# Three mixed cells of eight in the up projection of a hybrid decoder layer, with the embedding's input split in the attention stage and two plain cells at the end of the first pair

## The chip, the cores and the metric

The kernel runs on one core of one Trainium2 chip. The metric is the device time of one execution in microseconds, the median of several runs. Below, PE is the TensorE engine (the matmuls), DVE is VectorE, ACT is ScalarE, POOL is GpSimd, and SP is the engine that issues the weight transfers.

## The reference

One layer of a decoder is computed in float32 for 256 tokens of width 2048:

```python
a = RMSNorm(h)
z, xBC, dt, q, k, v = split(a @ W_in)
h = h + concat(ssd_heads(z, xBC, dt), windowed_attention(q, k, v)) @ W_out
g, u = split(causal_dwconv3(RMSNorm(h) @ W_up))          # W_up: 2048 x 11264
h = h + (SiLU(g) * u) @ W_down                           # W_down: 5632 x 2048
h = h + sigmoid(RMSNorm(h) @ W_pg) * RMSNorm(p @ W_pe)   # p: 256 x 256, W_pe: 256 x 2048
```

The change lies in the line of `W_up`, and in the product `p @ W_pe` (the embedding), which the kernel computes early and keeps in memory.

## The kernel before

**Products.** A float32 product is made of three matmuls: each operand is split into a high part (a cast, on ACT) and a low part (source minus high, a subtraction on DVE), and hi·wh, hi·wl and lo·wh are accumulated in one PSUM bank. Each matmul has a 128x128 stationary piece of the activations and a 128x512 piece of the weights. Such a triple is called a run here.

**Weights.** They come in pieces of 512 KB (128 partitions x two k-tiles x 512 columns) on SP's queue into seven raw buffers. ACT casts a piece to `wh` (L205), DVE subtracts it to `wl` (L206); four such pairs are kept, and in the feed-forward stage a fifth. A raw buffer is free when both have read it, a pair when PE has used it.

**Order.** The order of PE's instructions is as the code is written (a manual schedule around it). The order on DVE, ACT, POOL and SP is set by a scheduler when the kernel is built, and each of these engines then works its rows in that order: a row that waits holds up all rows behind it.

**Stages.** The input projection with the SSD heads; the attention, whose work is handed out in numbered slots (`at`) between the chunks of the projection and of the output projection; then the feed-forward stage. This one begins with the embedding: its input `p` is loaded, split into `ph` and `pl`, and `embed(n)` (four of them, 12 matmuls each) multiplies it by `W_pe`; DVE copies each result out (L896) and it is stored. Between them stand `norm(n)` (scaling of h) and `left(n)` (transposes on PE at L932, and the split left operands of four k-tiles: for plain cells at L209, for mixed ones the sums at L943).

**Pairs and cells.** The up projection runs in 11 pairs, `up(c)`: 512 columns of g and 512 of u, each summed over 2048 rows, which are cut in eight cells `kp` of 256 rows. A *plain* cell is 8 runs (24 matmuls) and needs two weight pieces split. A *mixed* cell does the same 2x2 block product with seven block products instead of eight (sums of blocks, after Winograd): 7 runs (21 matmuls), but before that four subtractions 128x512 on DVE to make `ta` and `tb` from two raw pieces (L962), and three and a half pieces to split (`g`, `v` of half size, `ta`, `tb`). Cells 0 and 4 are mixed, the others plain.

**Banks.** A pair uses all eight PSUM banks: P1, P5, P6, P7 only for mixed cells, Q22 only for plain ones, Q2, Q3, Q4 for both. After the last mixed cell the P banks are combined in SBUF (L1029 to L1033), after the last plain cell the four Q banks are added (L1035). A bank can be used by the next pair once DVE has read it. Then `finish` turns the result (a copy on ACT L1000, a transposing transfer, a copy on ACT L1003), and the short convolution (ACT L307, DVE L309), SiLU and the product follow; all that runs beside the next pair.

**Between pairs.** `down` (the product with `W_down`) of an earlier group of pairs stands between two pairs from the third on; between pairs 0 and 1, and between 1 and 2, nothing stands. Pair 0 is special: `left` is made inside it (`boundary`), and its plain cells come first, so its order is 1, 2, 3, 5, 6, 7, 0, 4. The other pairs go 0 to 7.

## Time and profile before

| what | value |
|---|---|
| runs | 1433.77 us median of 3 (1432.09 to 1439.97) |
| the profiled execution | 1435.36 us, of which the span in the trace is 1433.6 us |
| TensorE clock granted, mean over the span | 0.995 of full |
| PE busy | 1414.3 us, 6461 matmuls |
| DVE busy | 1110.3 us, 1480 instructions |
| ACT busy | 901.6 us, 1196 instructions |
| feed-forward stage begins | 603.10 us is the start of the last matmul of the output projection |
| pairs 2 to 10 | from about 723 us on |

Times in the trace are microseconds from the start of the span. A row of a timeline gives start, busy time, engine, line, operation, output and inputs, and in brackets how long the engine was idle before it and which instruction ended the wait. A row of a group gives the total busy time and the mean time of one in ns. A row of a stretch gives, for PE, PE's weight loads, DVE, ACT and POOL, the busy time and the count, then the mean granted clock of PE, the share of the DMA engines and GB/s. Instructions on one engine overlap a little, so the pitch of neighbours (start to start) is shorter than the duration of one.

### The profile page before, as it was taken

Reading aid. Unit: us, or ns where it says so; the run is one execution under the profiler, and the core shown is the slowest. Engines: PE = TensorE matmul, PEld = TensorE weight load, DVE = VectorE, ACT = ScalarE, POOL = GpSimd, SP = SyncE. Lnnn points to the kernel's source line nnn. Section 1 sums busy time; section 2 is a strip of 40 time slices with the busy share of each in tenths; the row PEclk is TensorE's granted clock in tenths of the full one; section 3 lists DMA queues with packets and bytes.
Section 4 is the critical chain, followed back from the end, with each engine's and each line's share of the span. In section 5 each row is a group of like instructions: output and inputs, shape, how many; then the busy total and the mean of one; then the engine's idle time right before and its main releaser. Section 6 shows DMA issues by size and latency. Waiting matters only on the chain.

```text
span 1433.6 us, 18135 instructions
## 1 busy us (share of the span) xinstructions
PE 1414.3 (99%) x6461; PEld 1156.6 (81%) x6461; DVE 1110.3 (77%) x1480; ACT 901.6 (63%) x1196; POOL 131.5 (9%) x114
## 2 busy tenths in 40 slices
PE   9999999999999999898999999999999999999998
PEld 7888888888787778686888888888888888888887
DVE  7678876776778888688898887878788787877764
ACT  6675555644677666565787575666757576665653
POOL 0002010018344522000000000000000000000000
PEclk9999999999999999999999999999999999999999
DMA  9656655548777778565678677686766777676672
GB/s 340 232 173 207 208 184 184 162 151 231 191 208 200 205 224 227 180 229 157 191 221 219 226 213 210 217 228 199 220 216 185 239 215 214 204 222 214 219 253 67
DMA packets 164907, 296.80 MB, mean 207 GB/s; under 512 B 93201, under 2 KB 96081, under 8 KB 164177
## 3 DMA queue, kind: packets, MB, share of 16 engines
q1 hardware_dynamic: 162800, 289.94, 67.7%
q10 hardware_dynamic: 2016, 5.72, 1.1%
q8 instruction: 50, 0.82, 0.2%
q14 instruction: 41, 0.33, 0.1%
HBM read 270.41 MB, written 4.23 MB: 192 GB/s over the span
## 4 chain that ended last, share of the span: by engine, by line
PE 64%; DVE 4%; ACT 1%; issue 1%; DMA 0%; POOL 0%; DVEq 0%; ACTq 0%
PE b L951 10%; PE b L950 10%; PE b L952 10%; PE b L241 8%; PE b L243 8%; PE b L242 8%; PE acc L241 3%; PE acc L242 3%; PE acc L243 3%; DVE wl L206 2%; PE tr L802 1%; ACT wh L205 0%; PE sc L761 0%; DMA w<-in_w_up_dram 0%; PE b L293 0%
## 5 line engine op out<-in xcount | busy, mean ns | idle before, releaser
L206 DVE TENSOR_TENSOR wl<-w,wh 128x1024 fp32r<-128x1024 f32 (+1 forms) x473 | 582.7, 1240 | 208.2 <-ACT wh L205 207.3
L205 ACT CAST wh<-w 128x1024 fp32r<-128x1024 f32 (+1 forms) x473 | 488.5, 1044 | 320.5 <-PE b L952 110.7
L950 PE MATMUL b<-wh,ah 128*128 128x512 f32 x484 | 189.6, 392 | 3.9 <-DVE c L1032 2.0
L951 PE MATMUL b<-wl,ah 128*128 128x512 f32 x484 | 188.9, 390 | 0.3 <-DVE wl L206 0.3
L952 PE MATMUL b<-wh,al 128*128 128x512 f32 x484 | 189.0, 390 | 0.0
L242 PE MATMUL acc<-wl,ah 128*128 128x512 f32 x448 | 176.9, 395 | 0.0
L241 PE MATMUL acc<-wh,ah 128*128 128x512 f32 x448 | 175.8, 395 | 0.0
L243 PE MATMUL acc<-wh,al 128*128 128x512 f32 x448 | 175.6, 392 | 0.0
L241 PE MATMUL b<-wh,gh 128*128 128x512 f32 x352 | 137.1, 390 | 0.0
L243 PE MATMUL b<-wh,gl 128*128 128x512 f32 x352 | 137.0, 389 | 0.0
L242 PE MATMUL b<-wl,gh 128*128 128x512 f32 x352 | 136.9, 389 | 0.0
L950 PEld LDWEIGHTS b<-wh,ah 128*128 128x128 f32 x484 | 91.3, 189 | 24.5 <-ACT wh L205 2.4
L951 PEld LDWEIGHTS b<-wl,ah 128*128 128x128 f32 x484 | 91.2, 189 | 19.5 <-DVE wl L206 0.7
L952 PEld LDWEIGHTS b<-wh,al 128*128 128x128 f32 x484 | 91.2, 188 | 19.0
L241 PE MATMUL acc<-wh,yh 128*128 128x512 f32 x256 | 101.2, 395 | 0.3 <-DVE h L417 0.3
L242 PE MATMUL acc<-wl,yh 128*128 128x512 f32 x256 | 99.8, 390 | 0.0
L243 PE MATMUL acc<-wh,yl 128*128 128x512 f32 x256 | 99.6, 390 | 0.0
L241 PEld LDWEIGHTS acc<-wh,ah 128*128 128x128 f32 x448 | 84.2, 188 | 18.9 <-issue 1.1
L242 PEld LDWEIGHTS acc<-wl,ah 128*128 128x128 f32 x448 | 84.2, 188 | 18.4 <-issue 1.1
L243 PEld LDWEIGHTS acc<-wh,al 128*128 128x128 f32 x448 | 84.2, 188 | 17.8 <-issue 0.7
L243 PEld LDWEIGHTS b<-wh,gl 128*128 128x128 f32 x352 | 66.1, 188 | 13.7
L242 PEld LDWEIGHTS b<-wl,gh 128*128 128x128 f32 x352 | 66.1, 188 | 13.7
(289 smaller groups left out, 2256.7 us busy)
## 6 DMA issues: line engine op xcount, KB each, us to landing
w<-in_w_up_dram SPq DMA_DIRECT2D x176, 512.0 KB, 4.4
w<-in_w_in_dram SPq DMA_DIRECT2D x126, 512.0 KB, 4.1
w<-in_w_down_dram SPq DMA_DIRECT2D x88, 512.0 KB, 4.3
w<-in_w_out_dram SPq DMA_DIRECT2D x64, 512.0 KB, 4.1
w<-in_w_pg_dram SPq DMA_DIRECT2D x32, 512.0 KB, 4.4
seg<-scr SPq DMA_DIRECT2D x8, 512.0 KB, 5.0
xt<-in_xT_dram SPq DMA_DIRECT2D x16, 128.0 KB, 6.9
h<-in_x_dram SPq DMA_DIRECT2D x2, 1024.0 KB, 7.7
```

Of the source, the lines that this page charges most:

```text
L205: S.copy(hi, src)
L206: V.tensor_tensor(out=lo, in0=src, in1=hi.bitcast(F32), op=ALU.subtract)
L241: PE.matmul(acc[b], lhsT=hi, rhs=wh[:, i, :], start=(k == 0), stop=False)
L242: PE.matmul(acc[b], lhsT=hi, rhs=wl[:, i, :], start=False, stop=False)
L243: PE.matmul(acc[b], lhsT=lo, rhs=wh[:, i, :], start=False, stop=(k == total - 1 or (b == NB - 1 and k + 1 == whole)))
L802: PE.matmul(v3(o[e * HD : (e + 1) * HD, kv * 2 * P : (kv + 1) * 2 * P], 2), lhsT=v[kb][:, vs], rhs=pT[e][:, :, kb, :], start=(kb == 0), st ...
L950: PE.matmul(acc, lhsT=hi, rhs=wh, start=start, stop=False)
L951: PE.matmul(acc, lhsT=hi, rhs=wl, start=False, stop=False)
L952: PE.matmul(acc, lhsT=lo, rhs=wh, start=False, stop=stop)
```

## The change

Four edits belong together.

1. `MIXED` is (0, 3, 5): three of eight cells are mixed, in all pairs.
2. The embedding's input is loaded and split in slot 88 of the attention stage, into the tiles `ah3` and `al3` of the activations' pool, which the plain cells 1 and 2 take over later. The convolution's coefficients `fcw` move to the pool of constants, and their load is written at the same place.
3. Pair 0 takes the plain cells 1, 2, 4, then the mixed ones 0, 3, 5, then the plain ones 6 and 7; `boundary` goes by the place in the list of plain cells. A class `Banks` counts the runs for the start and stop of each bank.
4. The two buffers `half0` and `half1` become one buffer `half`.

```diff
-MIXED = (0, 4)
+MIXED = (0, 3, 5)
...
+        em = []
+
+        def embedding():
+            pt_ = sb(act, [P, KG, T], "ah3")[:, :KW, :]
+            nc.scalar.dma_start(pt_, pT)
+            nc.scalar.dma_start(fcw, ffn_cw)
+            t = sb(act, [P, KG, T], "al3", F32R)
+            em.extend((t[:, :KW, :], t[:, KW:, :]))
+            split(pt_, *em)
+
+        at[88] = embedding
...
-    pp = ctx.enter_context(tc.tile_pool(name="fcw", bufs=1))
-    fcw = sb(pp, [P, 88 * 4], "fcw")
-    nc.scalar.dma_start(fcw, ffn_cw)
-    fill(pp)
...
-        pt_ = sb(fp, [P, 4, T], "uc", bufs=1)[:, :2, :]
-        nc.scalar.dma_start(pt_, pT)
-        ph, pl = (sb(fp, [P, KW, T], f"p{e}0", F32R, 1) for e in "hl")
-        split(pt_, ph, pl)
+        ph, pl = em
...
+        class Banks:
+
+            def __init__(self):
+                self.t = [bank() for _ in range(8)]
+                self.left = [len(MIXED)] * 4 + [len(MIXED) + KW * len(plain)] * 3 + [KW * len(plain)]
+                self.used = set()
...
-            order = (P1, P5, P7, P6, Q4, Q2, Q3) if first and fresh else (P1, Q2, Q3, P5, P7, P6, Q4)
+            order = (P1, Q2, Q3, P5, P7, P6, Q4) if acc.used else (P1, P5, P7, P6, Q4, Q2, Q3)
...
-                half = sb(fp, [P, 2 * NC], f"half{b}", U16, 1)
+                half = sb(fp, [P, 2 * NC], "half", U16, 1)
...
             if before:
-                kps.sort(key=lambda kp: kp in MIXED)
-            seen, left_over = {True: 0, False: 0}, {True: len(MIXED), False: len(kps) - len(MIXED)}
+                kps = plain[:-2] + list(MIXED) + plain[-2:]
...
-                if m and last:
+                if kp == MIXED[-1]:
...
         def boundary(kp):
-            if kp == 1:
+            if kp == plain[0]:
...
-            elif kp in (2, 5):
-                n = 2 + kp // 5
-                norm(n)
-                left(n)
+            for n in range(2, KG):
+                if kp == plain[n - 1]:
+                    norm(n)
+                    left(n)
```

Since the scheduler sets DVE's order, the rows of DVE at three places show what the diff doesn't. In the changed program the lines are some numbers higher (L206 is L207, L896 is L902, L1030 to L1035 are L1038 to L1043).

At the start of the feed-forward stage, DVE before: the rows from the embedding's copies on (L896) to the two low parts of cell 1's left operand (`al` at L209).

```order
640 L896 COPY c_1138_5466<-b_5446 128x512
641 L896 COPY c_1139_5469<-b_5447 128x512
642 L206 TENSOR_TENSOR wl_5644<-w_5641,wh_5643 128x1024
643 L896 COPY c_1145_5492<-b_5472 128x512
644 L896 COPY c_1146_5495<-b_5473 128x512
645 L206 TENSOR_TENSOR wl_5662<-w_5659,wh_5661 128x1024
646 L209 SCALAR_TENSOR_TENSOR al_1150_5507<-b_5501,gains_94,ah_1149_5506 128x256
647 L943 TENSOR_TENSOR uc_5517<-uc_5517 128x128
648 L896 COPY c_1161_5551<-b_5531 128x512
649 L943 TENSOR_TENSOR uc_5517<-uc_5517 128x128
650 L896 COPY c_1162_5554<-b_5532 128x512
651 L209 SCALAR_TENSOR_TENSOR al_1150_5507<-b_5501,gains_94,ah_1149_5506 128x256
```

The same place on DVE now, with the waits: `ta` and `tb` are those of the first mixed cell, `al` is the tile `al3` that `ph` and `pl` lay in.

```order
652 L980 TENSOR_TENSOR tb_5744<-w_5741,ta_5743 128x512 [waits DVE_49]
653 L207 TENSOR_TENSOR wl_5645<-w_5642,wh_5644 128x1024 [waits DMAHW0_49,Activation_49]
654 L902 COPY c_1144_5489<-b_5467 128x512 [waits DMAHW7_49,PE_49]
655 L207 TENSOR_TENSOR wl_5663<-w_5660,wh_5662 128x1024 [waits DMAHW1_49,Activation_49]
656 L949 TENSOR_TENSOR uc_5511<-uc_5511 128x128 [waits Activation_49]
657 L902 COPY c_1159_5545<-b_5525 128x512 [waits DMAHW1_49,PE_49]
658 L980 TENSOR_TENSOR tb_5744<-w_5739,tb_5744 128x512 [waits DVE_49]
659 L949 TENSOR_TENSOR uc_5511<-uc_5511 128x128 [waits Activation_49]
660 L210 SCALAR_TENSOR_TENSOR al_1148_5501<-b_5495,gains_94,ah_1147_5500 128x256 [waits PE_49]
661 L902 COPY c_1160_5548<-b_5526 128x512 [waits DMAHW2_49]
662 L207 TENSOR_TENSOR wl_5706<-w_5703,wh_5705 128x1024 [waits Activation_49]
```

The first `al` stands behind five weight splits since the last addition to h, where it stood behind five before as well, but `vl` and four subtractions of the first mixed cell have come ahead of it; and it now waits for PE, which is the last matmul of `embed(3)`, the last reader of the tile.

At the end of pair 0 DVE had, before, these rows, in which L1030 to L1033 and L1035 free pair 0's banks, `wl_6063` to `wl_6117` are pieces for pair 1's cells, and `ta_6172` begins the next mixed cell:

```order
699 L1030 TENSOR_TENSOR c_1242_5942<-c_1240_5940,b_5413 128x512
700 L206 TENSOR_TENSOR wl_6036<-tb_6018,wh_6035 128x1024
701 L1031 TENSOR_TENSOR c_1241_5941<-c_1242_5942,b_5415 128x512
702 L1035 TENSOR_TENSOR c_1240_5940<-c_1240_5940,b_5416 128x512
703 L206 TENSOR_TENSOR wl_6063<-w_6060,wh_6062 128x1024
704 L206 TENSOR_TENSOR wl_6081<-w_6078,wh_6080 128x1024
705 L1032 TENSOR_TENSOR c_1242_5942<-c_1242_5942,b_5414 128x512
706 L1035 TENSOR_TENSOR c_1241_5941<-c_1241_5941,b_5418 128x512
707 L206 TENSOR_TENSOR wl_6117<-w_6114,wh_6116 128x1024
708 L1033 TENSOR_TENSOR c_1243_5943<-c_1242_5942,b_5415 128x512
```

Now the P banks of pair 0 (L1038 to L1041) are read between the weight splits of its last two plain cells (`wl_5928`, `wl_5946`) and the first pieces of pair 1 (`wl_6036`, `ta_6029`, `tb_6030`):

```order
698 L207 TENSOR_TENSOR wl_5928<-w_5925,wh_5927 128x1024
699 L1038 TENSOR_TENSOR c_1237_5882<-c_1235_5880,b_5407 128x512
700 L207 TENSOR_TENSOR vl_6040<-w_6027,vh_6039 128x512
701 L980 TENSOR_TENSOR tb_6030<-w_6027,ta_6029 128x512
702 L207 TENSOR_TENSOR wl_5946<-w_5943,wh_5945 128x1024
703 L207 TENSOR_TENSOR wl_6036<-w_6025,wh_6035 128x1024
704 L1039 TENSOR_TENSOR c_1236_5881<-c_1237_5882,b_5409 128x512
705 L980 TENSOR_TENSOR tb_6030<-w_6025,tb_6030 128x512
706 L207 TENSOR_TENSOR wl_6044<-ta_6029,wh_6043 128x1024
707 L1040 TENSOR_TENSOR c_1237_5882<-c_1237_5882,b_5408 128x512
708 L1043 TENSOR_TENSOR c_1235_5880<-c_1235_5880,b_5410 128x512
```

The combination of the P banks has moved ahead, beside two plain cells of the same pair. At the end of pair 1 (its banks are `b_6018` to `b_6024`), DVE now has these rows, in which `wl_6446` belongs to the first mixed cell of pair 2, `wl_6473` to `wl_6527` to the two plain cells behind it and `ta_6546`, `tb_6547` to its second mixed cell:

```order
764 L1043 TENSOR_TENSOR c_1325_6274<-c_1325_6274,b_6021 128x512
765 L207 TENSOR_TENSOR wl_6446<-tb_6428,wh_6445 128x1024
766 L980 TENSOR_TENSOR ta_6546<-w_6544,w_6542 128x512
767 L980 TENSOR_TENSOR ta_6546<-w_6544 128x512
768 L1040 TENSOR_TENSOR c_1327_6276<-c_1327_6276,b_6019 128x512
769 L1043 TENSOR_TENSOR c_1326_6275<-c_1326_6275,b_6023 128x512
770 L207 TENSOR_TENSOR wl_6473<-w_6470,wh_6472 128x1024
771 L207 TENSOR_TENSOR wl_6491<-w_6488,wh_6490 128x1024
772 L980 TENSOR_TENSOR tb_6547<-w_6544,ta_6546 128x512
773 L207 TENSOR_TENSOR wl_6527<-w_6524,wh_6526 128x1024
774 L1041 TENSOR_TENSOR c_1328_6277<-c_1327_6276,b_6020 128x512
775 L207 TENSOR_TENSOR wl_6509<-w_6506,wh_6508 128x1024
```

There the reading of pair 1's banks (L1040, L1041, and L1043 in two rows behind the last one shown) has moved behind work for pair 2. On ACT's queue the load of `fcw`, which stood behind the attention's last work before, is the first transfer after `gains` at the very start of the program.

More of the change, by code (lines that the diff above doesn't have):

```diff
@@ L193, in hybrid_layer @@
     posi = sb(const, [P, NB], "posi", I32)
+    fcw = sb(const, [P, 88 * 4], "fcw")
     fill(mc)
@@ L946, in left, with __getitem__, run, cell_mixed @@
                 left_parts[kp] = hi, lo
-        def run(acc, lhs, rhs, start, stop):
-            (hi, lo), (wh, wl) = lhs, rhs
-            PE.matmul(acc, lhsT=hi, rhs=wh, start=start, stop=False)
-            PE.matmul(acc, lhsT=hi, rhs=wl, start=False, stop=False)
-            PE.matmul(acc, lhsT=lo, rhs=wh, start=False, stop=stop)
         P1, P6, P7, P5, Q2, Q4, Q3, Q22 = range(8)
         A11, A12, A22, S1, S2, S3, S4 = range(7)
-        def cell_mixed(acc, kp, c, first, last, fresh):
+        class Banks:
[3 more added lines that the diff above has]
+                self.used = set()
+            def __getitem__(self, m):
+                return self.t[m]
+            def run(self, m, lhs, rhs):
+                (hi, lo), (wh, wl) = lhs, rhs
+                self.left[m] -= 1
+                PE.matmul(self.t[m], lhsT=hi, rhs=wh, start=m not in self.used, stop=False)
+                PE.matmul(self.t[m], lhsT=hi, rhs=wl, start=False, stop=False)
+                PE.matmul(self.t[m], lhsT=lo, rhs=wh, start=False, stop=not self.left[m])
+                self.used.add(m)
+        def cell_mixed(acc, kp, c):
             wg, wu = (load_raw(w_up[n, kp]) for n in (c, NPAIR + c))
@@ L977, in cell_mixed, with cell_plain @@
                     r = [t[:, i, :] for t in w]
-                run(acc[m], (hi[:, f, :], lo[:, f, :]), r, first and (fresh or m in (P1, P5, P6, P7)), last and (m in (P1, P5, P6, P7) or not fresh))
-        def cell_plain(acc, kp, c, first, last, fresh):
+                acc.run(m, (hi[:, f, :], lo[:, f, :]), r)
+        def cell_plain(acc, kp, c):
             h, l = left_parts[kp]
@@ L987, in cell_plain @@
                         bs = slice(b * P, (b + 1) * P)
-                        run(
-                            acc[m],
-                            (h[:, i, bs], l[:, i, bs]),
-                            [t[:, i, :] for t in w],
-                            first and (not fresh or m == Q22) and i == 0,
-                            last and (fresh or m == Q22) and i == KW - 1,
-                        )
+                        acc.run(m, (h[:, i, bs], l[:, i, bs]), [t[:, i, :] for t in w])
         def finish(c, us):
@@ L1013, in up @@
         def up(c, before=None):
-            acc = [bank() for _ in range(8)]
+            acc = Banks()
             kps = list(range(KT // KW))
             if before:
-                kps.sort(key=lambda kp: kp in MIXED)
-            seen, left_over = {True: 0, False: 0}, {True: len(MIXED), False: len(kps) - len(MIXED)}
+                kps = plain[:-2] + list(MIXED) + plain[-2:]
             for kp in kps:
-                m = kp in MIXED
-                if before and not m:
+                if before and kp in plain:
                     before(kp)
-                first, last = not seen[m], seen[m] == left_over[m] - 1
-                (cell_mixed if m else cell_plain)(acc, kp, c, first, last, not before)
-                seen[m] += 1
-                if m and last:
+                (cell_mixed if kp in MIXED else cell_plain)(acc, kp, c)
+                if kp == MIXED[-1]:
                     c0, y, x, z = (staged(i) for i in range(4))
```

## The prediction, made before the changed kernel was run

> **What bounds the kernel now.** I read the page first: shares, then the costliest groups.
>
> ```profile
> PE 1414.3 (99%) x6461; PEld 1156.6 (81%) x6461; DVE 1110.3 (77%) x1480; ACT 901.6 (63%) x1196; POOL 131.5 (9%) x114
> L206 DVE TENSOR_TENSOR wl<-w,wh 128x1024 fp32r<-128x1024 f32 (+1 forms) x473 | 582.7, 1240 | 208.2 <-ACT wh L205 207.3
> L205 ACT CAST wh<-w 128x1024 fp32r<-128x1024 f32 (+1 forms) x473 | 488.5, 1044 | 320.5 <-PE b L952 110.7
> ```
>
> PE sets the time, so a matmul taken away counts at its pitch; DVE has 23% left on the mean. Where PE isn't full, the stretches tell (busy times in the order PE, PEld, DVE, ACT, POOL, then the granted clock).
>
> ```profile
> 600.00:620.00 20.00, 15.89 (x63) 12.42 (x62) 13.13 (x20) 9.78 (x16) 0.71 (x1) 0.83 0.64 199
> 607.00:613.30 6.30, 5.71 (x13) 4.25 (x14) 3.23 (x8) 1.93 (x5) 0.71 (x1) 0.51 0.64 207
> 660.00:700.00 40.00, 34.62 (x139) 26.65 (x138) 32.97 (x49) 31.39 (x39) 0.00 (x0) 0.91 0.63 174
> 667.00:682.00 15.00, 9.62 (x29) 5.97 (x28) 13.80 (x19) 10.42 (x11) 0.00 (x0) 0.77 0.86 229
> 700.00:721.00 21.00, 20.68 (x93) 16.78 (x91) 21.00 (x26) 12.70 (x15) 0.00 (x0) 1.00 0.67 213
> 721.00:785.00 64.00, 64.00 (x282) 52.99 (x283) 55.22 (x75) 50.69 (x60) 0.00 (x0) 1.00 0.85 226
> 721.00:1325.00 604.00, 604.00 (x2665) 500.26 (x2666) 494.03 (x625) 400.37 (x453) 0.00 (x0) 1.00 0.73 216
> ```
>
> From 721 us on PE has no gap at all. It has two holes: at the start of the feed-forward stage and at the end of pair 0. The timeline shows the first:
>
> ```profile
> 603.03 1.28 DVE L417 TENSOR_TENSOR h<-h,acc 128x512 f32<-128x512 f32 x2
> 603.10 0.39 PE L243 MATMUL acc<-wh,yl 128*128 128x512 f32 x1
> ...
> 605.49 2.36 DVE L206 TENSOR_TENSOR wl<-w,wh 128x1024 fp32r<-128x1024 f32 x2 [1.19 <-ACT wh L205]
> 606.94 0.60 ACT L205 CAST ph<-uc 128x512 fp32r<-128x512 f32 x1
> 607.60 0.79 PE L241 MATMUL b<-wh,ph 128*128 128x512 f32 x1 [4.11 <-ACT ph L205]
> ```
>
> The embedding's matmul waits 4.11 us for the cast of its own input; then its 13 matmuls in 5.71 us run at a granted clock of 0.51, 0.44 us each. The second hole, PE and then DVE:
>
> ```profile
> 667.09 0.39 PE L950 MATMUL b<-wh,ah 128*128 128x512 f32 x1
> 667.32 0.39 PE L951 MATMUL b<-wl,ah 128*128 128x512 f32 x1
> 670.37 0.50 PE L950 MATMUL b<-wh,ah 128*128 128x512 f32 x1 [1.38 <-DVE c L1035]
> 673.33 0.47 PE L950 MATMUL b<-wh,ah 128*128 128x512 f32 x1 [1.98 <-DVE c L1032]
> 675.56 0.79 PE L950 MATMUL b<-wh,ah 128*128 128x512 f32 x1 [0.48 <-DVE c L1033]
> 678.65 0.80 PE L950 MATMUL b<-vh,ah 128*128 128x512 f32 x1 [1.44 <-DVE c L1035]
> 680.10 0.63 PE L950 MATMUL b<-wh,ah 128*128 128x512 f32 x1
> 669.63 0.68 DVE L1035 TENSOR_TENSOR c<-c,b 128x512 f32<-128x512 f32 x1
> 670.23 2.35 DVE L206 TENSOR_TENSOR wl<-w,wh 128x1024 fp32r<-128x1024 f32 x2
> 672.50 0.68 DVE L1032 TENSOR_TENSOR c<-c,b 128x512 f32<-128x512 f32 x1
> ```
>
> Pair 1 starts on banks that DVE still has to read, and DVE does two splits for pair 1 first. Cell 1 of pair 1 begins at 680.10. The pitch of PE is 0.23 us (667.09, 667.32); 29 matmuls at 0.23 would fill 6.6 of the 15 us from 667 to 682: the hole costs about 8.4 us, waits and slow clock together.
>
> **The change, part by part.** All terms are against the profiled execution, 1435.36 us with a span of 1433.6; that is 1.6 above the median of 1433.77, which I subtract at the end.
>
> *Third mixed cell.* 24 matmuls become 21 in each of 11 pairs: 33 x 0.227 = -7.5 us on PE. DVE and ACT pay, with these rows (counts and means over the kernel):
>
> ```profile
> L962 DVE TENSOR_TENSOR ta<-w,w 128x512 f32<-128x512 f32 x22 | 15.1, 688 | 13.1 <-DMA w<-in_w_up_dram 13.0
> L206 DVE TENSOR_TENSOR wl<-ta,wh x22: 1212/1217/1234, 650.7 to 1246.4; 128x1024 fp32r<-128x1024 f32 x22
> L206 DVE TENSOR_TENSOR vl<-w,vh x22: 680/684/687, 637.1 to 1241.8; 128x512 fp32r<-128x512 f32 x22
> L309 DVE SCALAR_TENSOR_TENSOR cv<-uc,fcw,cv 128x254 f32<-128x254 f32 x88 | 40.8, 477 | 0.0
> L962 DVE TENSOR_TENSOR ta<-w,w 128x512 f32<-128x512 f32 x2 | 1.4, 692 | 4.9 <-DMA w<-in_w_up_dram 4.9
> 661.41 0.68 DVE L962 TENSOR_TENSOR ta<-w,w 128x512 f32<-128x512 f32 x1
> 662.01 0.68 DVE L962 TENSOR_TENSOR ta<-w 128x512 f32<-128x512 f32 x1
> 663.82 1.22 DVE L206 TENSOR_TENSOR wl<-w,wh 128x1024 fp32r<-128x1024 f32 x1
> 664.95 1.22 DVE L206 TENSOR_TENSOR wl<-ta,wh 128x1024 fp32r<-128x1024 f32 x1
> 700.75 0.48 DVE L309 SCALAR_TENSOR_TENSOR cv<-uc,fcw,cv 128x254 f32<-128x254 f32 x1
> 701.14 2.35 DVE L206 TENSOR_TENSOR wl<-w,wh 128x1024 fp32r<-128x1024 f32 x2
> ```
>
> Four subtractions of 0.69, one more split of 1.22 and half a one of 0.68: +4.65 us of DVE a pair. In a pair with `down` behind it (721 to 785) that makes 55.2 + 4.65 = 59.9 of 64.0 - 0.7 = 63.3 us: hidden, but the slack falls from 8.8 to 3.4.
>
> *Embedding split early.* The 4.1 us wait and the slow clock go: the first matmul can follow the last of the output projection (603.1 + 0.2), at 603.3 instead of 607.6. What is late next is cell 1's left operand. By DVE's new order, at the pitches above (start to start 1.14 for 1024 columns, 0.60 for 512, 0.39 for the convolution's), there stand between 605.5, where the splits start now, and its `al`: 5 splits (5.7), 7 copies (4.2), 4 subtractions (2.4), `vl` (0.6), and small ones, about 1.5: 14.4 us, so 619.9, written by 620.3. PE, with 48 matmuls (10.9) and twice 8 transposes (0.8 each, the rows below), would be there at 603.3 + 12.5 = 615.8 and wants it two matmuls later: it waits 4 us. The second k-tile's `al` stands a copy, a split and two short rows later, about 2.3 us, and PE waits 2 us again. Cell 1 then ends at about 627 (622.7 and 19 matmuls), where the next transposes began at 628.56 before:
>
> ```profile
> 628.56 1.04 PE L932 MATMUL b<-ident,cv 128*128 128x128 f32 x8
> 629.35 0.47 PE L950 MATMUL b<-wh,ah 128*128 128x512 f32 x1
> ```
>
> That is -1.6; bounds: 0 if the clock falls again, -6.7 (4.1 and 2.6 of slow clock: 13 matmuls x 0.2) if DVE is in time. I take -1.5. The cover on ACT isn't the bound: its casts come before these rows. The wait for `embed(3)` itself costs nothing, since its last matmul ends before 616.
>
> *Pair 0's end.* P banks are read beside two plain cells (48 x 0.227 = 10.9 us). Only L1043 on the last cell's banks stays close, some 0.7 us: -8.4 + 0.7 = -7.7; bounds -8.4 and, if the same rows still come late, -4.
>
> *Pair 1's end.* Here no `down` gives DVE time. A pair's DVE rows at pitch: before 2 mixed (3 splits, `vl`, 4 subtractions: 6.4 each) + 6 plain (2.28) + 8 bank rows (4.8) + 16 convolution rows (0.39 each), product and `gl` (8.6): 40, against (42 + 144) x 0.227 = 42.2 on PE. Now 3 x 6.4 + 5 x 2.28 + 13.4 = 44.0 against (63 + 120) x 0.227 = 41.5. DVE is the bound of pair 1, by 2.5 us (already before, from 700 to 721, it was busy all 21 us), and its order puts `wl` of pair 2's cells 0, 1 and 2 ahead of L1040, L1041 and the last L1043: from the last split of pair 1 to that row stand 20 rows, about 18 us, while PE has half a plain cell and a mixed one, 7.5 us, before it needs those banks. If DVE arrives with its usual lead of two or three splits, 10 us of lateness becomes about 7. I take +7; bounds 0 and +10 (slow clock on top). Before, there was only this:
>
> ```profile
> 720.96 0.50 PE L951 MATMUL b<-wl,ah 128*128 128x512 f32 x1 [0.32 <-DVE wl L206]
> ```
>
> *Load of `fcw`* first at the start: 176 KB at 340 GB/s of the first slice (the page's GB/s line) is 0.5 us before the first weights; +0.4, bounds 0 and 0.5. One buffer `half`: the second copy waits for the first transfer, beside other work, 0.
>
> ```profile
> GB/s 340 232 173 207 208 184 184 162 151 231 191 208 200 205 224 227 180 229 157 191 221 219 226 213 210 217 228 199 220 216 185 239 215 214 204 222 214 219 253 67
> ```
>
> Sum: -7.5 - 1.5 - 7.7 + 7 + 0.4 = -9.3. 1435.4 - 9.3 = 1426.1 profiled; less 1.6, **1424.5**.
>
> The Trainium skill, "TensorE: Matmul & The Clock Gate", HAM clock gate, says that the clock is halved after an idle window of about 3.4 us and comes back after a busy one. This trace agrees after the 4.11 us wait (0.51), but it also shows 0.77 from 667 to 682, where no single wait is over 1.98. By the page alone only the 4 us wait would be followed by slow matmuls, an estimate of 1.7 us more (half of 3.4); by the row both new holes may be, and that is held in the bounds above.
>
> **Rivals.** (a) *All is covered*: DVE runs ahead at both places. For it: no gap of PE from 721 to 1325. Against it: the sums above, and the present hole at 670, made by two splits. Time: -7.5 - 6.7 - 8.4 + 0.4 = -22, 1411.5; with pair 1's end alone covered 1417.5, with the embedding alone 1419.5.
>
> (b) *DVE becomes the bound in the pairs with `down`*: slower. Its place is `ta`, which waits for raw pieces: 4.9 us over two cells, 2.45 each. If a third such wait comes on the path and isn't slack, DVE needs 59.9 + 3 x 2.45 = 67.3 of 63.3, and decides: from 3.4 us of waits on. 9 pairs x 4 = +36, 1460; with a quarter of it, 1433, with half, 1442.5. For it: the DMA share of 0.85 in 721 to 785. Against it: these waits come while PE is full, so DVE was ahead.
>
> (c) *The new holes eat the gain*: both with slow clock, embedding 0, pair 1's end +10, pair 0's end -4: -7.5 - 4 + 10 + 0.4 = -1.1, 1432.7, no change.
>
> (d) *The change doesn't move the hole at pair 0*, since DVE's rows stay late: -4 instead of -7.7 in the sum, 1428.
>
> **How the numbers follow.** A measurement of this kernel tells 0.5%, 7.2 us: faster is under 1426.6, slower over 1440.9. My forecast 0.45 (own range 1419 to 1429), (a) 0.2, (c) and (d) 0.22, (b) 0.13, of which 0.08 is slower. Faster: 0.32 of the forecast, all of (a), 0.08 of the rest: 0.60; slower 0.09; within 0.31. The range, 1411 to 1438, leaves out half of (b) and the tails.
>
> **What would show it.** The first embedding matmul at about 603.3 with no wait for `ph`; then waits for `al` (now L210) of 2 to 5 us; PE full through the start of pair 1 at about 670 (680.1 before); waits of PE on DVE's L1040, L1041 or L1043 at pair 1's end, some 7 us; from pair 2 on no gap, and pairs shorter by 0.7. Gaps in every pair, ended by `wl` or `ta`, would prove (b); none at 616 and 710, (a). I am wrong in mechanism if PE waits anywhere for ACT instead of DVE.

## The result and the profile after

The changed kernel takes 1443.78 us (median of 7 runs, 1440.94 to 1447.31) where the kernel before takes 1437.05 (7 runs): the ratio is 1.0055, 95% interval 1.0039 to 1.0071. The change makes the kernel slower by about half a percent. Forecast were 1424.5 us and a range of 1411 to 1438; the prediction was wrong in size and in sign. In the tables below the ratios leave out a few single slow executions, as one of e3's five and one of p1's five, which the medians count. Each set of runs has its own measurement of the kernel before (medians 1435.71 to 1437.05 us), so between runs of different sets the ratio is the safer comparison.

The profiled execution took 1447.31 us with a span of 1445.6, the longest of the seven; against the profiled execution before (1435.36, span 1433.6) the traces differ by 12 us, the medians by 6.7. What follows reads the places from the traces and the sizes from the medians.

The page of the changed kernel, first part, has 33 matmuls less and 69 instructions of DVE more:

```profile
PE 1415.1 (98%) x6428; PEld 1153.6 (80%) x6428; DVE 1158.4 (80%) x1549; ACT 919.1 (64%) x1219; POOL 130.2 (9%) x113
```

The waits of PE in the changed kernel (engine, line, what it waited for: us in total, times, longest):

```profile
PE b L971 <- DVE wl L207: 7.7, 7, 2.5
PE b L972 <- DVE al L210: 5.6, 2, 4.7
PE b L970 <- DVE c L1041: 3.5, 1, 3.5
...
PE acc L242 <- DVE nm L774: 2.0, 1, 2.0
PE b L970 <- DVE c L1043: 1.5, 2, 0.8
```

The wait for `ph` (4.1 us) is gone, and of the waits at the end of pair 0 (5.3 us before) one of 0.77 us for L1043 is left, as the prediction has it. `al` and L1041 are the two new holes that the prediction names. `nm` is in the attention stage, which it does not speak of, and of the seven waits for `wl` six stand from pair 2 on, where it says "no gap". The seventh and longest stands inside pair 1, with a slow matmul behind it:

```profile
705.61 0.79 PE L971 MATMUL b<-wl,ah 128*128 128x512 f32 x1 [2.49 <-DVE wl L207]
```

The stretches show the two named holes: from 619 to 634 PE is busy 9.35 of 15 us at a granted clock of 0.66, from 719 to 731 7.39 of 12 at 0.77.

```profile
619.00:634.00 15.00, 9.35 (x26) 6.50 (x24) 13.27 (x23) 9.16 (x16) 0.00 (x0) 0.66 0.62 212
719.00:731.00 12.00, 7.39 (x24) 4.95 (x23) 11.85 (x15) 7.30 (x8) 0.00 (x0) 0.77 0.58 182
792.00:1283.00 491.00, 486.87 (x2135) 401.03 (x2134) 434.10 (x553) 330.61 (x374) 0.00 (x0) 1.00 0.72 214
```

The third row is pairs 3 to 10: PE, which had no gap there before, now stands idle 4.1 us.

Start times of the same matmuls in the two traces give the loss stage by stage (the last column is what the prediction's terms make of the stage, with 0.7 us a pair for the third cell):

| matmul | before, us | changed, us | stage: measured | stage: forecast |
|---|---|---|---|---|
| last of the output projection | 603.10 | 606.26 | +3.2 | +0.4 |
| first transposes after cell 1 of pair 0 | 628.56 | 634.56 | +2.8 | -1.5 |
| first of pair 1 | 667.09 | 672.39 | -0.7 | -0.7 |
| first of pair 1's cell 1 | 680.10 | 678.22 | -7.2 | -7.7 |
| first of pair 2 | 718.21 | 719.10 | +2.8 | -0.7 |
| first of pair 3 | 782.79 | 791.77 | +8.1 | +6.3 |
| last of pair 10 | 1272.16 | 1283.22 | +2.1 | -5.4 |
| end of the span | 1433.6 | 1445.6 | +0.9 | 0 |

Pair 0's hole and pair 1's end came out nearly as worked out. Four stages did not: the attention, cell 1, the inside of pair 1, and pairs 3 to 10. The attention's row is the least certain of them: in the traces of this document that have no early split, the last matmul of the output projection starts anywhere from 601.56 (e1) to 606.39 us (m3).

### The profile page after: what moved, and what is told of

The parts are those of the page before. It is cut to its first block, busy times and chain, and to the rows that moved or that the text cites. A ratio compares the mean times of both kernels' runs of the same rounds, so it can differ in the third digit from the quotient of the medians.

```text
span 1445.6 us, 18183 instructions
## 1 busy us (share of the span) xinstructions
PE 1415.1 (98%) x6428; PEld 1153.6 (80%) x6428; DVE 1158.4 (80%) x1549; ACT 919.1 (64%) x1219; POOL 130.2 (9%) x113
## 4 chain that ended last, share of the span: by engine, by line
PE 73%; DVE 12%; DMA 7%; issue 4%; ACT 3%; POOL 0%; SPq 0%; DVEq 0%; ACTq 0%; POOLq 0%
PE acc L242 10%; PE acc L243 10%; PE acc L244 10%; PE b L971 8%; PE b L972 8%; PE b L970 8%; DVE wl L207 6%; PE b L243 5%; PE b L244 5%; PE b L242 5%; DMA flip<-half 4%; DVE cv L310 2%; PE acc L351 2%; ACT wh L206 2%; DMA w<-in_w_up_dram 2%
## 5 line engine op out<-in xcount | busy, mean ns | idle before, releaser
L207 DVE TENSOR_TENSOR wl<-w,wh 128x1024 fp32r<-128x1024 f32 (+1 forms) x462 | 576.2, 1259 | 184.5 <-ACT wh L206 181.7
L206 ACT CAST wh<-w 128x1024 fp32r<-128x1024 f32 (+1 forms) x462 | 475.8, 1044 | 275.4 <-PE acc L244 98.0
L971 PE MATMUL b<-wl,ah 128*128 128x512 f32 x374 | 149.4, 400 | 6.6 <-DVE wl L207 6.5
L972 PE MATMUL b<-wh,al 128*128 128x512 f32 x374 | 148.8, 398 | 5.6 <-DVE al L210 5.6
L970 PE MATMUL b<-wh,ah 128*128 128x512 f32 x374 | 149.2, 399 | 3.9 <-DVE c L1041 3.5
L971 PE MATMUL b<-wl,ph 128*128 128x512 f32 x264 | 103.0, 390 | 1.2 <-DVE wl L207 1.2
L970 PE MATMUL b<-wh,ph 128*128 128x512 f32 x264 | 103.0, 390 | 0.0
L972 PE MATMUL b<-wh,pl 128*128 128x512 f32 x264 | 102.7, 389 | 0.0
L971 PEld LDWEIGHTS b<-wl,ah 128*128 128x128 f32 x374 | 72.1, 193 | 24.3 <-DVE wl L207 9.6
L972 PEld LDWEIGHTS b<-wh,al 128*128 128x128 f32 x374 | 72.1, 193 | 21.9 <-DVE al L210 6.8
```

The lines of the kernel that those rows point to most:

```text
L206: S.copy(hi, src)
L207: V.tensor_tensor(out=lo, in0=src, in1=hi.bitcast(F32), op=ALU.subtract)
L970: PE.matmul(self.t[m], lhsT=hi, rhs=wh, start=m not in self.used, stop=False)
L971: PE.matmul(self.t[m], lhsT=hi, rhs=wl, start=False, stop=False)
L972: PE.matmul(self.t[m], lhsT=lo, rhs=wh, start=False, stop=not self.left[m])
```

## The experiments

### One part of the change at a time

Three runs hold one of the three large parts each, a fourth the change without the early split. All have `fcw` in the pool of constants and one buffer `half`, as the changed kernel has.

```diff
e1:  MIXED = (0, 3, 5); embedding split in the feed-forward stage; pair 0: plain cells, then mixed ones
e2:  MIXED = (0, 4); at[88] = embedding; pair 0: plain cells, then mixed ones
e3:  MIXED = (0, 4); embedding split in the feed-forward stage; pair 0: plain[:-2] + MIXED + plain[-2:]
e4:  the changed kernel, embedding split in the feed-forward stage
```

The third cell alone.

> The third mixed cell alone: the embedding is split at the start of the feed-forward stage as before, and pair 0 takes its plain cells first and its mixed ones last as before. Theory (the third mixed cell makes DVE the bound; this loses more than the 7.5 us that PE gains): the hole at the end of pair 0 stays at 8 us or more, a new hole of 5 to 8 us at the end of pair 1, single waits of PE for wl in some of pairs 3 to 10 of some 5 us in all; the time 3 to 10 us above before. Rival (the loss of the change comes from the embedding's new place, the third cell is worth what PE gains): 6 to 8 us below before.

The early split alone.

> The embedding's early split alone, with two mixed cells and pair 0's order of before. Cell 1's left operand lies in another tile than the embedding's input here. Theory (the split in slot 88 delays the attention stage by about 3 us, and DVE's queue delays cell 1's left operand whatever the tile): the last matmul of the output projection 2 to 3 us later than before, PE waits 2 to 5 us for al, and the time is within 3 us of before. Rival 1 (the reuse of the embedding's tile is what makes al late): no wait for al over 1 us, and 3 to 6 us below before. Rival 2 (the attention's delay has another cause, such as the two slower score products): the last matmul of the output projection at 603 to 604.

The order alone.

> Pair 0's order alone (1, 2, 3, 5, then the mixed cells 0 and 4, then 6 and 7), with two mixed cells and the embedding's split as before. Theory (reading the P banks beside two plain cells removes the hole at the end of pair 0, and with two mixed cells DVE isn't the bound of pair 1): 6 to 8 us below before, no wait over 1 us at the ends of pair 0 and pair 1. Rival (the hole moves to the end of pair 1, because DVE has no time to make it up before a pair with the down projection): waits of 4 to 8 us at pair 1's end, within 3 us of before.

All but the early split.

> The changed kernel with the embedding's split put back to the start of the feed-forward stage. Theory (the early split loses 3 us in the attention stage and 3 us at cell 1, more than the 4 us wait that it removes): 3 to 7 us below the changed kernel, about 1438, no wait for al over 1 us, the last matmul of the output projection at 603. Rival (the early split gains its 4 us net and the loss lies in the pairs alone): 2 to 5 us above the changed kernel, 1446 to 1449.

| run | median, us | ratio to before (95%) |
|---|---|---|
| e1, third cell | 1445.64 | 1.006 (1.0045 to 1.0075) |
| e2, early split | 1441.52 | 1.0037 (1.0024 to 1.005) |
| e3, order | 1444.19 | 1.0052 (1.0036 to 1.0068) |
| e4, without early split | 1446.80 | 1.007 (1.0055 to 1.0085) |

Every part alone is slower than before, and the order alone, of which its expectation had a gain or nothing, loses 0.52%, 7.5 us. The third cell alone came out where its theory put it, 3 to 10 us above before; what follows shows that this was luck, since the loss has another cause. The early split alone lost 5 us where at most 3 were expected, and its waits for `al` are 0.7 us at the longest, not 2 to 5: with two mixed cells and another tile, neither of the two causes of the late `al` that are separated below is there in full. The parts don't add up to the whole; so something that all four share loses. Two rows show where to look. In the run of the order, with only two mixed cells, single waits for `wl` stand in pairs 5 to 10, as in the changed kernel; the timeline has the largest:

```profile
923.91 0.50 PE L974 MATMUL b<-wl,ah 128*128 128x512 f32 x1 [1.89 <-DVE wl L207]
```

and the list of ACT's waits has, in the kernel before and then in the run of the order:

```profile
ACT uc L1003 <- DMA flip<-half: 5.5, 5, 1.7
```

```profile
ACT uc L1018 <- DMA flip<-half: 32.9, 17, 4.5
```

ACT waits six times as long for the transposing transfers of `finish`. Of what the four runs share, only the buffer `half` touches these transfers. e4 points the same way: without the early split the kernel takes 1446.8 us against 1443.78 of the whole change, where about 1438 was expected. That is the case of its rival, that the loss lies in the pairs; the intervals of the two ratios overlap.

### The buffer alone, and the buffer given back

```diff
f1, on the kernel before:
-                half = sb(fp, [P, 2 * NC], f"half{b}", U16, 1)
+                half = sb(fp, [P, 2 * NC], "half", U16, 1)
f5 = e3 and f6 = e2, with:
-                half = sb(fp, [P, 2 * NC], "half", U16, 1)
+                half = sb(fp, [P, 2 * NC], f"half{b}", U16, 1)
g1 = the changed kernel, with:
-                half = sb(fp, [P, 2 * NC], "half", U16, 1)
+                half = sb(fp, [P, 2 * NC], "half", U16, 1) if b == 0 else sb(fp, [P, NC], "c0" if c < NPAIR else "c1", bufs=1).bitcast(U16)
```

With three mixed cells a second `half` does not fit beside the left operands, so g1 uses for it the tile of `c0` (later `c1`), which has just been copied and holds nothing needed.

> The kernel before with only one edit: one buffer half for both token blocks instead of two. Theory (the single buffer chains the two transposing transfers of a finish one behind the other; ACT, which works its rows in order, waits for flip, and the casts behind it come late): ACT's waits for flip rise from 5.5 to some 30 us, single waits of PE for wl appear in pairs 3 to 10, and the time is 4 to 9 us above before. Rival (the buffer costs nothing; what the four parts have in common that loses is the load of fcw at the start, or the new order of the runs): within 2 us of before.

> Pair 0's order alone, with two mixed cells, the embedding's split as before, and two buffers half. Theory (the single buffer was the loss in the run of the order alone): 5 to 9 us below before, about 1429, no waits of PE for wl over 0.5 us from pair 3 on. Rival (the order itself costs what it gains): within 2 us of before, with waits at pair 1's end.

> The embedding's early split alone, with two mixed cells, pair 0's order of before and two buffers half. Theory: 5 to 7 us below the run of the early split with one buffer, so 0 to 3 us below before; the 1 to 2 us wait of the attention for nm stays, since the split's rows cause it. Rival (the early split is a loss of its own): 2 to 5 us above before.

> The changed kernel with a second buffer for half that takes no new memory: for the second token block the copy goes into the tile of c0 or c1, which is free once the first block has been copied. Theory (the single buffer is the loss): 6 to 10 us below the changed kernel, about 1435, ACT's waits for flip under 12 us, no single waits of PE for wl over 1 us from pair 3 on; what is left against before is the third mixed cell's gain less the waits at cell 1 and at pair 1's end. Rival (with three mixed cells DVE is the bound in every pair, whatever the buffer): within 3 us of the changed kernel, the waits for wl stay.

| run | median, us | ratio to before (95%) | ACT's waits for flip, us | the same with one buffer |
|---|---|---|---|---|
| f1, before with one buffer | 1444.57 | 1.0063 (1.0042 to 1.0083) | 29.9 | - |
| f5, order | 1433.53 | 0.9981 (0.9967 to 0.9995) | 8.7 | 1444.19 |
| f6, early split | 1437.84 | 1.0007 (0.9996 to 1.0018) | 10.5 | 1441.52 |
| g1, whole change | 1438.67 | 1.002 (1.0006 to 1.0033) | 12.8 | 1443.78 |

The buffer alone costs 8.9 us on the kernel before, which is the upper edge of what was expected, and by the ratios 0.30 to 0.71% (4 to 10 us) in the three pairs of runs that differ in nothing else. Read against f1 (1.0063) instead of the kernel before, none of the parts e1 (1.006), e2 (1.0037) and e3 (1.0052) shows a loss. Giving the buffer back brought f6 and g1 less than expected: 4 us instead of 5 to 7, and 5 us instead of 6 to 10. The timeline of ACT in f1, at the end of a pair, shows the mechanism:

```profile
892.07 1.04 ACT L1000 COPY half<-c 128x1024 uint16<-128x1024 uint16 x1
...
896.29 1.16 ACT L1003 COPY uc<-flip 128x1024 uint16<-128x1024 uint16 x1
897.36 1.04 ACT L1000 COPY half<-c 128x1024 uint16<-128x1024 uint16 x1
898.31 2.02 ACT L205 CAST wh<-w 128x1024 fp32r<-128x1024 f32 x2
903.18 1.17 ACT L1003 COPY uc<-flip 128x1024 uint16<-128x1024 uint16 x1 [2.85 <-DMA flip<-half]
904.25 1.04 ACT L1000 COPY half<-c 128x1024 uint16<-128x1024 uint16 x1
905.20 1.05 ACT L205 CAST wh<-w 128x1024 fp32r<-128x1024 f32 x1
```

The same place in the kernel before:

```profile
887.31 1.98 ACT L1000 COPY half<-c 128x1024 uint16<-128x1024 uint16 x2
...
891.70 1.17 ACT L1003 COPY uc<-flip 128x1024 uint16<-128x1024 uint16 x1
892.77 1.04 ACT L1000 COPY half<-c 128x1024 uint16<-128x1024 uint16 x1
893.72 1.05 ACT L205 CAST wh<-w 128x1024 fp32r<-128x1024 f32 x1
894.67 1.16 ACT L1003 COPY uc<-flip 128x1024 uint16<-128x1024 uint16 x1
```

With two buffers the first two copies into `half` follow one another, and the second transfer runs while ACT does other rows; the two `uc` copies come without a wait. With one buffer each `half` copy stands behind the transfer of the one before, and a `uc` copy waits 2.85 us with the next `half` copy and the cast of the next weight behind it. DVE's next row is a split of that weight, and it waits on the cast:

```profile
906.28 1.23 DVE L206 TENSOR_TENSOR wl<-w,wh 128x1024 fp32r<-128x1024 f32 x1 [2.24 <-ACT wh L205]
```

That is time which DVE, with 55.2 of 64 us busy, doesn't find again in every pair: PE waits for `wl` at 927.45 us (1.47 us), at 1250.35 (2.14 us) and at six more places, 6.8 us in all, where the kernel before has no gap. That the buffer makes these waits is shown, since f1 differs in nothing else; which late row of ACT leads to which wait of PE, some 20 us later, is not.

In g1 the gaps of pairs 3 to 10 are gone:

```profile
855.00:918.00 63.00, 63.00 (x280) 52.16 (x279) 56.67 (x74) 43.37 (x50) 0.00 (x0) 1.00 0.72 218
792.00:1283.00 491.00, 490.92 (x2166) 406.20 (x2165) 436.16 (x555) 337.40 (x379) 0.00 (x0) 1.00 0.73 217
```

So three mixed cells with DVE at 56.67 of 63 us are covered where a down projection follows; rival (b) of the prediction is refuted with two buffers. But g1 did not come to 1435, and f5, the order, gains 2.7 us by the ratio where 5 to 9 were expected: what g1 still loses lies before pair 3.

### Attention, cell 1 and the end of pair 1

g4 is the changed kernel with two buffers and without the early split; k1 is g1 with the embedding's input in the tiles of mixed cell 5; h3 and h5 are g4 and k1 with the subtractions on POOL.

```diff
k1:
-            pt_ = sb(act, [P, KG, T], "ah3")[:, :KW, :]
+            pt_ = sb(act, [P, KG * T], "ah2").rearrange("p (k t) -> p k t", k=KG)[:, :KW, :]
-            t = sb(act, [P, KG, T], "al3", F32R)
+            t = sb(act, [P, KG * T], "al2", F32R).rearrange("p (k t) -> p k t", k=KG)
h3, h5:
-                V.tensor_tensor(out=o, in0=x0, in1=x1, op=ALU.subtract)
+                G.tensor_tensor(out=o, in0=x0, in1=x1, op=ALU.subtract)
```

> The changed kernel with the second half buffer in c0 or c1, and the embedding's split put back to the start of the feed-forward stage: three mixed cells and the new order of pair 0 are left. Theory (the early split is worth about nothing net: it takes away a 4 us wait and puts 2 us into the attention stage and 5 us before cell 1): within 2 us of the changed kernel with the second buffer, 1437 to 1441. Rival (the early split is the loss that is left): 3 to 5 us below it, 1434 to 1435.

> The changed kernel with the second half buffer, and with the embedding's input in the tiles of the mixed cell 5, which are needed only later, instead of those of cell 1. Theory (cell 1's left operand is late because of the rows ahead of it in DVE's queue, the wait for the last reader of the tile adds little): the wait for al falls from 5.3 us to 3 to 4.5, the time within 2 us of the changed kernel with the second buffer. Rival (the reuse of the tile is the cause): the wait falls under 1 us, and the time by 4 us or more.

> As the one without the early split, with the four subtractions of each mixed cell moved from DVE (VectorE) to POOL (GpSimd), which is idle in the pairs. Theory (what eats the third cell's gain is DVE's work in pairs 0 to 2): the waits for wl and for the bank rows in pairs 1 and 2, some 15 us, fall to under 7, and the time is 5 to 9 us below the kernel without the early split, under 1433. Rival (it is the order of DVE's rows, not their sum, or POOL is too slow or slows DVE's own rows): within 3 us of it or above it; then the subtractions take over 2 us each on POOL, or DVE's splits get longer than 1.22 us.

> The one before with the subtractions on POOL: the whole change, the second half buffer, the embedding in other tiles. Theory: four rows of 0.6 us less stand ahead of al, so PE's wait there falls to 2 us or less, and the waits in pairs 1 and 2 fall to under 7 us; 1429 to 1433, 5 us or more below before. Rival (POOL doesn't help): within 3 us of the run with other tiles.

| run | median, us | ratio to before (95%) |
|---|---|---|
| g4, without early split | 1438.34 | 1.0021 (1.0007 to 1.0035) |
| k1, other tiles | 1437.07 | 1.0008 (0.9997 to 1.0019) |
| h3, g4 with POOL | 1445.53 | 1.0064 (1.0043 to 1.0085) |
| h5, k1 with POOL | 1448.22 | 1.0069 (1.0047 to 1.0092) |

g4 against g1: the early split is worth nothing net (1438.34 and 1438.67, ratios 1.0021 and 1.002), as the theory had it. It takes the 4.1 us wait away and pays for it in the attention and before cell 1. k1 says what makes `al` late; PE's waits for it in g1 and then in k1:

```profile
PE b L972 <- DVE al L210: 5.3, 2, 4.3
```

```profile
PE b L972 <- DVE al L210: 4.1, 2, 2.2
```

The tile's reuse is about 1.2 us of it; the rest is put down to DVE's queue, as expected, and p2 below bears that out. The POOL runs are 7 and 11 us slower than their partners, as the rival said, and the reason shows in the durations. In h3 (the first and the third of a cell's four subtractions, then `vl` on DVE):

```profile
L983 POOL TENSOR_TENSOR ta<-w,w 128x512 f32<-128x512 f32 x33 | 95.6, 2898 | 374.7 <-DMA w<-in_w_up_dram 230.3 <-DVE wl L207 137.9 <-DVE c L1044 3.4
...
L983 POOL TENSOR_TENSOR tb<-w,ta 128x512 f32<-128x512 f32 x33 | 65.0, 1969 | 1.4 <-DVE wl L207 1.4
...
L207 DVE TENSOR_TENSOR vl<-w,vh 128x512 fp32r<-128x512 f32 x33 | 34.3, 1041 | 15.9 <-ACT vh L206 15.9
```

A subtraction of 0.69 us on DVE takes 1.7 to 2.9 on POOL on the mean, and beside it DVE's own `vl` goes from 0.68 to 1.04 us. The 132 subtractions were some 90 us of DVE's work; with them gone DVE is busy 1139.6 us in h3 instead of 1155.1 in g4, only 15.5 less. So h3 does not say that less work on DVE is no use; DVE was hardly relieved.

The same contact shows in the attention. The early split changed DVE's order there, and the timeline of DVE and then of POOL in the changed kernel shows a split of 3.15 us where one takes 1.22, beside a copy on POOL:

```profile
498.48 3.15 DVE L207 TENSOR_TENSOR wl<-w,wh 128x1024 fp32r<-128x1024 f32 x1
501.56 0.67 DVE L418 TENSOR_TENSOR h<-h,acc 128x512 f32<-128x512 f32 x1
502.15 0.22 DVE L774 TENSOR_TENSOR nm<-nm,nsink 128x4 f32<-128x4 f32 x1
```

```profile
497.95 2.60 POOL L713 COPY s<-flip 128x2048 uint16<-128x2048 uint16 x1
```

In the kernel before, a split and the same copy meet the other way round: the split starts first and keeps nearly its length, and the copy, which takes 2.1 us at its shortest, is the longer one.

```profile
497.47 1.31 DVE L206 TENSOR_TENSOR wl<-w,wh 128x1024 fp32r<-128x1024 f32 x1
```

```profile
497.64 3.14 POOL L712 COPY s<-flip 128x2048 uint16<-128x2048 uint16 x1
```

`nm`, behind the long split, is what PE's 2.00 us wait at 502.38 hangs on. e2, f6 and g1 have the same wait (1.5, 1.9 and 2.0 us) and the same long split; g4, without the early split, has none, and k1, where the split's tiles are others and DVE's rows fall otherwise, has none either. That the wait comes with this split in these tiles is shown. That POOL's copy stretches the split was not tried by taking the copy away, but the changed kernel's trace leaves little else: its 412 splits of this form with at most 0.3 us of POOL's work beside them all take under 1.25 us, and every longer one lies beside a row of POOL. The wait is 2.0 of the stage's 3.2 us; the rest is within what the traces differ by.

### A down projection behind pair 1

DVE had, by the prediction, 44 us of rows for 41.5 us of PE in pair 1, and no down projection to make it up: no *cover*, which here means a stretch of work of PE that asks little of DVE, so that DVE can catch up. m1 (g4), m2 (k1), m3 (f5) and m4 (before) put half of pair 0's there:

```diff
-SEGS = [2, 2, 2, 2, 2, 1]
+SEGS = [1, 2, 2, 2, 2, 2]
```

> Three mixed cells and the new order of pair 0, two buffers, no early split; the groups of pairs are 1, 2, 2, 2, 2, 2 instead of 2, 2, 2, 2, 2, 1, so that half of pair 0's down projection (10.9 us of PE) stands between pairs 1 and 2. Theory (pair 1's end waits because DVE has 44 us of rows for 41.5 us of PE and no cover behind): the waits in pair 2's first cells fall from 8.7 to under 2 us, and the time is 5 to 8 us below the same kernel without it, 1430 to 1433. Rival (DVE's order makes the hole wherever the down projection stands): waits of 5 us or more there, within 3 us.

> The whole change with the second buffer and the embedding in other tiles, and the groups 1, 2, 2, 2, 2, 2. Theory: 5 to 8 us below the same kernel without it, 1429 to 1432. Rival: within 3 us of it.

> Pair 0's order alone with two mixed cells and two buffers, and the groups 1, 2, 2, 2, 2, 2. Theory (3 us of waits at pair 1's end are left there to take): 2 to 4 us below the order alone, about 1430; if it is below the run with three mixed cells, then the third cell isn't worth its DVE time. Rival: no change, 1433.

> The kernel before with the groups 1, 2, 2, 2, 2, 2 alone. There is no hole at pair 1's end to take away, only 0.3 to 0.6 us. Theory: within 2 us of before, the hole at pair 0's end stays at 8 us. Rival (the regrouping gains something of its own, at the last pairs): 2 us or more below before.

| run | median, us | ratio to before (95%) | without the regrouping (ratio) |
|---|---|---|---|
| m1, three cells and order | 1437.79 | 1.0004 (0.9994 to 1.0015) | 1438.34 (1.0021) |
| m2, the whole, other tiles | 1435.28 | 0.9984 (0.9973 to 0.9996) | 1437.07 (1.0008) |
| m3, order, two cells | 1439.70 | 1.0018 (1.0006 to 1.003) | 1433.53 (0.9981) |
| m4, before | 1445.47 | 1.0058 (1.0042 to 1.0075) | 1436.76 (1) |

The place was right and the times were not: by the ratios m1 and m2 gain 2 to 3 us where 5 to 8 were expected, and m3 and m4 lose 5 and 8. In m1 PE is full through the end of pair 1, where the changed kernel was busy 7.39 of 12 us:

```profile
717.00:735.00 18.00, 18.00 (x81) 14.92 (x80) 17.24 (x24) 11.99 (x13) 0.00 (x0) 1.00 0.77 217
```

But the last group now has two pairs, and only two of four blocks of a down projection, about 22 us, stand between the last pair and its own down projection. That is not enough to hide `finish`, the convolution and the product:

```profile
1299.85 0.50 PE L242 MATMUL b<-wh,gh 128*128 128x512 f32 x1 [4.10 <-ACT gh L206]
```

With the slow matmuls behind it this costs 7 to 8 us in each of the four runs (from the last matmul of pair 10 to the end of the span, against the trace without the regrouping). In m4, which had nothing to gain at pair 1's end, it is most of the loss; that hole was in none of the expectations. m1 also keeps a wait of 1.87 us for ACT's `wh` inside pair 1, which g4 has too and which the down projection does not reach.

Two pairs of runs differ in the third cell alone (and in where the second buffer lies), and tell what it is worth. Without a down projection behind pair 1 it costs 0.40%, 5.7 us (g4 against f5); with one it gains 0.14%, 2.0 us (m1 against m3). The gain is not clear of the noise, but the difference between the two is: in these runs the third cell pays only where DVE has cover, and even then less than the 7.5 us that it takes off PE.

### Cover at both places

p1 is m2 with seven groups: one pair first, so that half of its down projection stands behind pair 1, and one pair last, so that the down projection of two whole pairs stands before its own. p2 also moves the embedding's eight copies out of PSUM from DVE to ACT.

```diff
p1, p2:
-SEGS = [2, 2, 2, 2, 2, 1]
+SEGS = [1, 2, 2, 2, 1, 2, 1]
p2:
-                V.tensor_copy(t, acc[b])
+                S.copy(t, acc[b])
```

> The whole change with the second buffer and the embedding in other tiles, and groups of 1, 2, 2, 2, 1, 2, 1 pairs: half of pair 0's down projection stands between pairs 1 and 2, and the last pair is a group of its own again, so that the down projection of two whole pairs stands behind it. Theory (the third cell's loss is where DVE has no cover): no wait of PE for gh, none over 1 us at pair 1's end, 5 to 8 us below the run with groups 1, 2, 2, 2, 2, 2, so 1427 to 1431 and 0.4 to 0.7% below before. Rival (DVE's load loses the same time elsewhere, for one group more brings eight more additions to h): within 3 us of it, with new waits for wl in pairs 5 to 9.

> As the one before, with the embedding's eight copies out of PSUM on ACT instead of DVE. Theory (rows ahead of al in DVE's queue): some five rows of 0.6 us fewer stand ahead of the first al, PE's wait there falls from 4 to 5 us to 2 or less, the time by 2 to 4 us. Rival (ACT then makes the high part ah late, since its casts wait behind the copies): PE waits for ah or al as long as before, and the time is within 2 us.

| run | median, us | ratio to before (95%) |
|---|---|---|
| p1 | 1430.83 | 0.9951 (0.9938 to 0.9964) |
| p2 | 1425.03 | 0.9916 (0.9903 to 0.993) |

In both runs no wait for `gh` is left and none for the banks of pair 1, and p1 is 4.5 us below m2, just short of the 5 to 8 that were expected: two waits of 1.8 us for `wl` stay, one inside pair 1 and one in the first cell of pair 2. p2 gains 5.8 us more, above the 2 to 4 that were expected. PE's waits in p1, then in p2:

```profile
PE b L972 <- DVE al L210: 4.9, 2, 3.1
...
PE b L970 <- ACT ah L209: 0.3, 1, 0.3
```

```profile
PE b L970 <- ACT ah L209: 2.9, 2, 2.6
...
PE b L972 <- DVE al L210: 1.1, 2, 0.7
```

With fewer rows ahead of it `al` is nearly in time; the high part, on ACT, is now the later one, as the rival said. The waits fall only from 5.2 to 4.0 us, but fewer slow matmuls follow: from 617 to 633 us p1's granted clock is 0.68, from 618 to 634 p2's is 0.89. By the traces pair 0 is 3.7 us shorter. Another 3.4 us come from pair 2, where p1's wait for `wl` is absent; why the copies should do that is not shown. The page of p2 has DVE's shares almost as in the changed kernel (81% against 80), with 19 to 21 us less time:

```profile
PE 1404.9 (99%) x6428; PEld 1147.9 (81%) x6428; DVE 1158.5 (81%) x1549; ACT 925.8 (65%) x1227; POOL 130.2 (9%) x113
```

The idea of the change holds: with the same cells and the same order of pair 0 the kernel is 0.84% faster than before, once the second buffer is back, the embedding's input lies in other tiles, down projections stand behind pair 1 and before the last one, and ACT copies the embedding. What the third cell alone is worth in p2 was not measured, nor what the seven groups, or ACT's copies, would give the kernel before.

## Why the prediction was wrong, point by point

- **Third cell, -7.5 on PE, hidden in pairs with a down projection.** Right: in g1 pairs 3 to 10 have no gap and each is 0.7 us shorter. Rival (b) is refuted, although the time came out on its side.
- **One buffer `half`: "the second copy waits for the first transfer, beside other work, 0".** This is the step that failed first: a cost put at nothing without a row that hides it. Alone it costs 8.9 us, in the changed kernel 5.1. f1 shows what was overlooked: ACT works its rows in order, so that a wait of a `uc` copy holds up the casts behind it, and DVE's splits behind these. The prediction's sign of a wrong mechanism, a wait of PE for ACT, does not catch this: the loss starts on ACT, but at PE it appears as waits for DVE's `wl`.
- **Embedding, -1.5.** The wait for `ph` went and the one for `al` came, by the mechanism that was named, 4.66 us where 4 was worked out. That the wait for `embed(3)` costs nothing was not right: other tiles take 1.2 us off (k1). Two terms were missing. The attention's +3.2 us was not in the sum at all, for the split's rows were followed only where they are needed, not in slot 88, where they change which rows of DVE and POOL meet. And the slow clock behind the waits (0.66 from 619 to 634) should have been in the value and not only in the bounds: with it the stage came to +2.8, where -1.5 was forecast. With two buffers the whole edit costs 0.3 us (g1 against g4) to 1 us (f6, 1.0007) instead of gaining 1.5, and neither is clear of the noise.
- **Pair 0's end, -7.7.** Right in the trace: -7.2. In f5, alone and with two buffers, it is worth only 2.7 us by the ratio: in that run's trace the two stages from the start of pair 1 to that of pair 2 are 8.9 us shorter than before, but pair 0 is 2.4 and pair 2 2.6 us longer, with new waits of 1.8 us for `ah` and `al` at cell 1 and of 2.5 us for `wl` in pair 2.
- **Pair 1's end, +7.** Right in place and cause, and somewhat small: +8.1 for the stage where +6.3 was forecast, and 2.5 us of waits for `wl` already inside pair 1. m1 confirms the cause, lack of cover: with 10.9 us of down projection there PE is full at pair 1's end.
- **`fcw` first, +0.4.** The first transposes at 55 us start 0.26 us later in the changed trace, inside the bounds; not tried alone.
- **The range.** 1438 as upper end took in the holes that were seen, with slow clock (c), and none that had been put at 0. A gain of 9.3 us was forecast and a loss of 6.7 measured, 16.0 us apart; 5.1 for the buffer (by the medians), 2.8 for the attention, 4.3 for cell 1, 3.5 inside pair 1 and 1.8 at its end (by one pair of traces) make 17.5. A further 3.3 us of the distance between 1424.5 and 1443.78 is no term of the change: the median of the kernel before went from 1433.77 us in three runs to 1437.05 in seven. g1, with the second buffer back, took 1438.67 us, just over the range: the buffer makes the miss of the range a clear one, the other four terms make the miss of its middle.

## What to carry to other kernels

An edit that only saves memory belongs in the sum too: a buffer that is shared by two transfers turns into a wait on the engine that fills it, and on an engine that works in order everything behind that wait is late. When an engine has more rows than the bound engine has time for a while, ask where the next stretch is that lets it catch up; moving such a stretch there paid here, moving rows to POOL did not, and moving rows to ACT did; the place that a stretch is taken from has to be looked at as well. When every part of a change alone loses, look for what the parts share.

## What the runs showed of the hardware

POOL and DVE slow each other here. With the subtractions on POOL, one of 128x512 took 1.7 to 2.9 us on the mean, and `vl` on DVE 1.04 us instead of 0.68; in the attention a DVE split that began during a POOL copy took 3.15 us instead of 1.22, and a POOL copy that began during a split 3.14 instead of 2.1. The Trainium skill, "GPSIMD Engine Reference", section 1, Specifications, states that the engine shares its SBUF interfaces with VectorE, with contention when a DVE instruction has two SBUF inputs; `vl` and the split are of that kind, and the traces agree.

The clock also fell behind single waits of 2 to 3 us. The Trainium skill, "TensorE: Matmul & The Clock Gate", Part 1, The HAM clock gate, has the clock halved after an idle window of about 3.4 us. Behind the 4.66 us wait in the changed kernel a matmul took 0.79 us instead of 0.39, first row, but in g1 the one behind a wait of 2.35 us took 0.77 too, second row; so the traces agree for the long wait and go beyond the page for the short one.

```profile
624.52 0.79 PE L972 MATMUL b<-wh,al 128*128 128x512 f32 x1 [4.66 <-DVE al L210]
```

```profile
723.04 0.77 PE L970 MATMUL b<-wh,ah 128*128 128x512 f32 x1 [2.35 <-DVE c L1040]
```

Not every wait does it: behind e3's wait of 1.89 us at 923.91 the first matmul took 0.50 us and the next one 0.40. For a sum it is safer here to price a cluster of waits of 1 to 4 us with slow matmuls behind it than without.
